# Moving GpSimd's share of the expert loop's weight subtracts to VectorE

## The chip, the cores and the metric

The kernel runs on one core of a Trainium2 chip. The metric is the device time of one execution in microseconds; the runs shown are three, with their median.

## The reference, cut to what matters

One layer of a streaming encoder over 2048 tokens of width 1024, in float32:

```
h = x + W_out [ Retention(n) ; RWKV7(n) ],   n = rms_norm(x) @ W_in
xn = rms_norm(h)
per token: one of 4 groups (argmax), then the 2 best of its 8 experts, weights = softmax(top 2) * group probability
y[token] += weight * ( silu(xb @ w_gate[e]) * (xb @ w_up[e]) ) @ w_down[e]      # 32 experts, 1024 -> 512 -> 1024
out = rms_norm_final(h + y)
```

The change lies in the part with the 32 experts, all of whose weights (6 MB each) are read once.

## The kernel before, in words

The kernel has three parts one after another: the mixers (to about 1500 us of the span), the tables of the routing, and the expert loop with the final norm behind it. Products are made of float32r parts: an operand is split into a high part, its cast to float32r, and a low part, the operand minus the high part, and three matmuls (high x high, low x high, high x low) are accumulated.

**Tiling of the expert loop** (lines 917 to 1223). Experts come in an order by size. Each has up to 128 tokens in a first block, and every second expert, by `more(e)`, a second block of 64 tokens. An expert is three stages: 0 the gate, 1 the up and 2 the down product; the list `stages` runs gate e, up e, down e-1, gate e+1 and so on. Each stage needs four weight chunks of 128 x 1024 float32 (512 KB).

**A chunk** is loaded by SP's queue into one of 8 buffers `raw` (line 903), cast on ScalarE (line 913) into the high half of one of 12 buffers `hl`, and the low half is written by a subtract `raw - hl` (line 914). Which engine casts and which subtracts is read from `SPLITS`, one string per kind of stage and one word per chunk: `a` or `v` (ScalarE or VectorE) for the cast, `p` or `v` (GpSimd or VectorE) for the subtract. The first six chunks are made ahead of the loop and don't use the table. Inside a stage four chunks are made, the last two of the next stage and the first two of the one behind it.

```
917: SPL = [[(V if a == "v" else SC, GP if b == "p" else V) for a, b in p.split()] for p in SPLITS]
913: (SC.copy if hi is SC else hi.tensor_copy)(hl[:, 0], raw)
914: lo.tensor_tensor(hl[:, 1], raw, hl[:, 0].bitcast(F32), op=ALU.subtract)
936: CH[si].append(chunk(*((SC, V) if first else SPL[stages[si][1]][c])))
```

**A stage**, in the order of the code: the first block's results of the stage before are taken from PSUM (`evict`); one chunk is made; the second block's matmuls of the stage before and its results (`rest`, where there is one); three chunks are made; additions that are due; then the stage's own matmuls in two halves. After each half of an up stage stand the transposes of half of the next expert's rows (`turn`, L1025), after those of a gate stage the transposes of the hidden rows (`hidden_turn`, L1125 for the first block, L1033 for the second). A transpose goes to one of two PSUM banks `tp`, which alternate; ScalarE casts it (L172) and VectorE subtracts (L173), and then the bank is free for the next transpose.

**GpSimd** has in the loop its share of the subtracts, the gathers of each expert's rows (`gather`, L1014, an indirect DMA into the one buffer `xb` of each block) and the additions of each expert's results to `h_d` (`add_rows`, L1147, an indirect DMA that adds). An addition waits for the one before it.

**Order.** In the loop the orders of TensorE, ScalarE, VectorE and GpSimd are those of the code (`manual_schedule`); SP's queue is ordered by a planner with priorities. A raw load is issued when the chunk eight places ahead of it has been made, and waits until that chunk's subtract has read the buffer.

Of the kernel before, what the change touches and what calls it, by code (L numbers as in the profile page):

```python
# [34 lines left out]
NFS = 6  # L35
FB = (2, 2, 2, 2, 2, 2, 2, 1, 1)
NRAW, NSP = 8, ((4, 0, 0), (4, 0, 0), (4, 0, 0))
SPLITS = ("av ap av vp", "av ap av av", "av ap av av")

N2 = 16  # L40

# [91 lines left out]
def build(tc, A, out, dbg=None, phases=3):  # L133
# [562 lines left out]
    if True:  # L696
# [219 lines left out]

        SPL = [[(V if a == "v" else SC, GP if b == "p" else V) for a, b in p.split()] for p in SPLITS]
        stages = [(0, 0), (0, 1)]
# [422 lines left out]
```

## Time and profile before

| | |
|---|---|
| three runs | 2427.48 us median (2424.75 to 2428.06) |
| profiled execution | 2430.18 us, of which the span 2428.4 |
| busy share of the span | TensorE 91%, VectorE 70%, GpSimd 48%, ScalarE 47% |
| weight subtracts (L914) | 259 on VectorE, 444.1 us; 125 on GpSimd, 332.6 us |
| weight casts (L913) | 353 on ScalarE, 352.0 us; 31 on VectorE |
| mean transfer rate | 187 GB/s over the span, 282 to 304 in most slices of the loop |
| granted TensorE clock | 0.951 mean |

Busy time counts an engine's instruction from its start to its end, and so also the time in which it stands still inside. A busy share of TensorE is not its peak. The three other engines take part in every stage of the expert loop, which runs from about 1567 to 2372 us of the span.

### The profile page before, as it was taken

The numbers are of one execution on the slowest core, as the hardware profiler recorded it, in microseconds if no ns is written. First come the engines' busy times: TensorE is split into PE (matmuls) and PEld (weight loads), VectorE is DVE, ScalarE is ACT, GpSimd is POOL, SyncE is SP. The second block draws the span as 40 slices with busy tenths as digits, with TensorE's granted clock in tenths as the row PEclk, the third lists the DMA queues.
The fourth block names the chain that finished last, engine by engine and source line by source line (L and its number), as shares of the span: only waits on it lengthen the run. The fifth ranks groups of instructions, "written<-read, shape, count | busy, mean of one in ns | idle before, by whom it ended". The sixth has DMA issues, their size and how long they took to land.

```text
span 2428.4 us, 36379 instructions
## 1 busy us (share of the span) xinstructions
PE 2207.2 (91%) x11816; PEld 1810.3 (75%) x11817; DVE 1710.4 (70%) x3500; ACT 1129.7 (47%) x1932; POOL 1161.3 (48%) x1530
## 2 busy tenths in 40 slices
PE   5999889998898989999879999699999999999990
PEld 4887778887787867877768888577777777777770
DVE  4477766878666877567775766768777787777875
ACT  4343433534434345333322222366666666666663
POOL 2036444354441575136542333466666666666650
PEclk9998999989999999999969999799999999999995
DMA  6643254432544335433234454488989999889978
GB/s 207 210 150 94 81 175 143 137 89 84 173 138 130 90 92 174 123 93 104 76 106 123 129 202 146 138 296 287 304 293 290 302 290 301 295 282 299 292 255 297
DMA packets 291298, 454.78 MB, mean 187 GB/s; under 512 B 93392, under 2 KB 164496, under 8 KB 291088
## 3 DMA queue, kind: packets, MB, share of 16 engines
q1 hardware_dynamic: 277136, 414.10, 51.6%
q0 software_dynamic: 13824, 37.80, 7.3%
q8 instruction: 94, 1.54, 0.3%
q14 instruction: 100, 0.82, 0.1%
q10 hardware_dynamic: 144, 0.52, 0.1%
HBM read 375.18 MB, written 81.85 MB: 188 GB/s over the span
## 4 chain that ended last, share of the span: by engine, by line
PE 47%; POOL 11%; DMA 7%; DVE 6%; issue 5%; ACT 3%; SPq 2%; POOLq 0%; DVEq 0%; ACTq 0%
PE acc L152 32%; PE pj L152 6%; POOL xl L488 5%; POOL tm L486 4%; PE pb L152 2%; PE tp L152 2%; ACT hl L913 1%; PE tp L1025 1%; DMA ln<-nl_d 1%; DVE hl L914 1%; PE psz L152 1%; DMA h_d<-yo,ti 1%; DMA xl_d<-xl 1%; PE psi L152 1%; SPq L490 1%
## 5 line engine op out<-in xcount | busy, mean ns | idle before, releaser
L152 PE MATMUL pj<-nT,whl 128*128 128x512 f32 x2496 | 626.4, 403 | 9.6 <-DVE nT L319 5.3
L914 DVE TENSOR_TENSOR hl<-raw,hl 128x1024 fp32r<-128x1024 f32 x259 | 444.1, 1745 | 142.6 <-ACT hl L913 142.6
L152 PEld LDWEIGHTS pj<-nT,whl 128*128 128x128 f32 x2496 | 464.9, 192 | 106.7 <-DVE nT L319 5.8
L152 PE MATMUL acc<-hl,xT 128*128 128x512 f32 (+1 forms) x2048 | 511.3, 402 | 0.0
L152 PEld LDWEIGHTS acc<-hl,xT 128*128 128x128 f32 (+1 forms) x2048 | 367.2, 183 | 100.8 <-ACT xT L172 0.2
L914 POOL TENSOR_TENSOR hl<-raw,hl 128x1024 fp32r<-128x1024 f32 x125 | 332.6, 2672 | 219.2 <-ACT hl L913 163.2
L913 ACT CAST hl<-raw 128x1024 fp32r<-128x1024 f32 x353 | 352.0, 1049 | 32.7 <-DMA raw<-in_wu_dram 26.9
L249 ACT CAST whl<-wraw 128x512 fp32r<-128x512 f32 x248 | 152.3, 618 | 304.8 <-PE pj L152 240.0
L250 DVE TENSOR_TENSOR whl<-wraw,whl 128x512 fp32r<-128x512 f32 x248 | 187.8, 760 | 146.1 <-ACT whl L249 141.7
L152 PE MATMUL acc<-hl,hT 128*128 128x512 f32 (+1 forms) x1024 | 249.6, 398 | 0.0
L486 POOL TENSOR_TENSOR tm<-xl,ln 128x60 f32<-128x60 f32 (+24 forms) x496 | 179.1, 361 | 105.6 <-DMA ln<-nl_d 69.0
L152 PEld LDWEIGHTS acc<-hl,hT 128*128 128x128 f32 (+1 forms) x1024 | 183.1, 181 | 51.7
L488 POOL TENSOR_TENSOR xl<-xl,tm 128x60 f32<-128x60 f32 (+24 forms) x496 | 187.5, 378 | 36.6
L152 PE MATMUL acc<-wo,mT 128*128 128x512 f32 x768 | 191.9, 401 | 0.0
L152 PEld LDWEIGHTS acc<-wo,mT 128*128 128x128 f32 x768 | 142.2, 191 | 28.5
L1147 POOL DMA_INDIRECT h_d<-yo,ti x48 | 107.5, 2239 | 53.8 <-DMA h_d<-yo,ti 40.5
L499 POOL COPY mbd<-pt 32x128 f32<-32x128 f32 x64 | 20.6, 321 | 226.5 <-DVE pt L464 199.4
L152 PE MATMUL pj<-whl,nT 128*128 128x256 f32 x768 | 118.6, 305 | 0.2 <-DVE gs L600 0.2
L152 PEld LDWEIGHTS pj<-whl,nT 128*128 128x128 f32 x768 | 105.9, 207 | 2.7 <-DVE gs L600 0.4
L464 DVE TENSOR_TENSOR pt<-pb,cst 64x512 f32<-64x512 f32 x128 | 88.0, 687 | 24.9 <-PE pb L152 23.1
L1014 POOL DMA_INDIRECT xb<-xt_d,ti x48 | 75.1, 1564 | 33.4 <-PE tp L1025 22.8
L172 ACT CAST xT<-tp 128x512 fp32r<-128x512 f32 x80 | 46.0, 589 | 80.7 <-PE tp L1025 65.7
(447 smaller groups left out, 3283.7 us busy)
## 6 DMA issues: line engine op xcount, KB each, us to landing
raw<-in_wg_dram SPq DMA_DIRECT2D x128, 512.0 KB, 4.7
raw<-in_wu_dram SPq DMA_DIRECT2D x128, 512.0 KB, 6.6
raw<-in_wd_dram SPq DMA_DIRECT2D x128, 512.0 KB, 6.7
wraw<-in_win_dram SPq DMA_DIRECT2D x208, 256.0 KB, 3.1
tr<-pf_d SPq DMA_DIRECT2D x80, 256.0 KB, 3.1
pf_d<-ev SPq DMA_DIRECT2D x52, 256.0 KB, 2.9
x<-in_xt_dram SPq DMA_DIRECT2D x32, 256.0 KB, 5.2
pf_d<-x SPq DMA_DIRECT2D x32, 256.0 KB, 4.2
```

The lines of the kernel that those rows point to most:

```text
L152: PE.matmul(o, l, r, start=start, stop=stop)
L172: SC.copy(dst_h, ps)
L249: SC.copy(hl[:, 0], raw)
L250: V.tensor_tensor(hl[:, 1], raw, hl[:, 0].bitcast(F32), op=ALU.subtract)
L464: V.tensor_tensor(pt[zs, i:i + 2, :, z ^ h], psp[h][zs].rearrange("p (f c) x -> p f c x", f=2), maskp[zs, None, None, :].to_broadcast([64, ...
L486: GP.tensor_tensor(tv, xl[:, 0:r, t:t + 1].to_broadcast([128, r, n]), ln[:, t:t + 1, t + 1:32].to_broadcast([128, r, n]), op=ALU.mult)
L488: GP.tensor_tensor(xl[:, 0:r, t + 1:32], xl[:, 0:r, t + 1:32], tv, op=ALU.add)
L490: SY.dma_start(xl_d[u].rearrange("l (r q) t -> q l r t", q=4)[q], xl[q * 32:(q + 1) * 32])
L913: (SC.copy if hi is SC else hi.tensor_copy)(hl[:, 0], raw)
L914: lo.tensor_tensor(hl[:, 1], raw, hl[:, 0].bitcast(F32), op=ALU.subtract)
L1014: return GP.indirect_dma_start(out=xbs[b], out_offset=None, in_=xt_d, in_offset=bass.IndirectOffsetOnAxis(ap=ti[b][:, e:e + 1], axis=0), b ...
L1147: GP.indirect_dma_start(out=h_d, out_offset=bass.IndirectOffsetOnAxis(ap=idx, axis=0), in_=y, in_offset=None, bounds_check=S + 127, comput ...
```

## The change

```
-SPLITS = ("av ap av vp", "av ap av av", "av ap av av")
+SPLITS = ("av av av av", "av av av av", "av av av av")
```

In all three kinds of stages the second chunk's subtract goes from GpSimd to VectorE. In a gate stage the fourth chunk's subtract does too, and its cast goes from VectorE to ScalarE. GpSimd keeps the gathers and the additions. Nothing else is edited.

## Rows read from the trace of the kernel before

**Rows 1.** Busy time in one stretch, 14 pairs of experts together; first line names the columns.
```profile
core 0: us, PE busy (x) PEld busy (x) DVE busy (x) ACT busy (x) POOL busy (x), PEclk, DMA share, GB/s
1596.79:2305.24 708.45, 691.29 (x3193) 532.71 (x3193) 531.75 (x462) 465.44 (x604) 461.82 (x196) 0.99 0.90 294
```
**Rows 2.** The same view, single pairs of experts.
```profile
1596.79:1645.64 48.85, 48.85 (x229) 37.86 (x229) 32.42 (x33) 33.03 (x44) 32.96 (x14) 1.00 0.87 280
1645.64:1695.75 50.11, 49.09 (x229) 37.80 (x229) 38.70 (x34) 34.19 (x45) 33.20 (x15) 1.00 0.90 296
1747.52:1798.92 51.40, 50.63 (x229) 38.87 (x229) 37.16 (x34) 33.09 (x43) 31.94 (x14) 0.97 0.90 298
1848.76:1900.52 51.76, 49.08 (x230) 37.79 (x229) 40.41 (x34) 33.42 (x44) 34.45 (x15) 1.00 0.92 285
2305.24:2355.00 49.76, 49.76 (x231) 38.54 (x231) 38.43 (x35) 33.06 (x44) 29.88 (x12) 1.00 0.93 305
```
**Rows 3.** Waits of TensorE in these 14 pairs: us in total, times, longest.
```profile
PE tp L1025 <- DVE hT L173: 17.2, 12, 2.7
```
**Rows 4.** Timeline of one gate and up stage: start, us, instruction, idle before it.
```profile
1837.14 4.76 POOL L914 TENSOR_TENSOR hl<-raw,hl 128x1024 fp32r<-128x1024 f32 x2
1838.54 3.89 ACT L913 CAST hl<-raw 128x1024 fp32r<-128x1024 f32 x4
1839.62 7.83 DVE L914 TENSOR_TENSOR hl<-raw,hl 128x1024 fp32r<-128x1024 f32 x3 [3.47 <-ACT hl L913]
1842.51 2.72 POOL L914 TENSOR_TENSOR hl<-raw,hl 128x1024 fp32r<-128x1024 f32 x1 [0.61 <-ACT hl L913]
1847.38 1.01 DVE L173 TENSOR_TENSOR hT<-tp,hT 128x512 fp32r<-128x512 f32 x2
1848.11 0.66 PE L1025 MATMUL tp<-ct,xb 128*128 128x128 f32 x4 [0.77 <-DVE hT L173]
```
**Rows 5.** The instructions of line 914: duration in ns, minimum/median/maximum.
```profile
L914 DVE TENSOR_TENSOR hl<-raw,hl x259: 1202/1220/7474, 1544.9 to 2360.9; 128x1024 fp32r<-128x1024 f32 x130
L914 POOL TENSOR_TENSOR hl<-raw,hl x125: 2347/2669/3427, 1570.4 to 2355.4; 128x1024 fp32r<-128x1024 f32 x125
```
**Rows 6.** Groups of VectorE in the 14 pairs: busy us, mean ns, idle before.
```profile
L914 DVE TENSOR_TENSOR hl<-raw,hl 128x1024 fp32r<-128x1024 f32 x224 | 390.9, 1774 | 126.3 <-ACT hl L913 126.2
L913 DVE CAST hl<-raw 128x1024 fp32r<-128x1024 f32 x28 | 19.2, 686 | 0.0
```
**Rows 7.** Timeline of the up and down stages before that.
```profile
1827.03 2.36 DVE L914 TENSOR_TENSOR hl<-raw,hl 128x1024 fp32r<-128x1024 f32 x2 [1.64 <-ACT hl L913]
1827.97 0.60 PE L1025 MATMUL tp<-ct,xb 128*128 128x128 f32 x4
1828.98 2.68 POOL L914 TENSOR_TENSOR hl<-raw,hl 128x1024 fp32r<-128x1024 f32 x1 [2.71 <-ACT hl L913]
1829.53 1.29 DVE L173 TENSOR_TENSOR xT<-tp,xT 128x512 fp32r<-128x512 f32 x2
1837.76 2.96 PE L152 MATMUL acc<-hl,xT 128*128 128x512 f32 x12
```
**Rows 8.** Timeline of ScalarE in the two down stages of a pair.
```profile
1806.61 2.13 ACT L913 CAST hl<-raw 128x1024 fp32r<-128x1024 f32 x2 [2.89 <-DMA raw<-in_wu_dram]
1837.26 1.39 ACT L1139 ACTIVATE yo<-acc,ws 128x512 f32<-128x512 f32 x2 [2.37 <-PE acc L152]
```
**Rows 9.** GpSimd's indirect DMAs: durations, two in the timeline, median us to landing.
```profile
L1147 POOL DMA_INDIRECT h_d<-yo,ti x48: 1432/2384/3606, 1619.7 to 2376.6; - x48
2371.20 1.43 POOL L1147 DMA_INDIRECT h_d<-yo,ti  x1 [5.25 <-DMA h_d<-yo,ti]
1835.43 1.67 POOL L1014 DMA_INDIRECT xb<-xt_d,ti  x1 [0.30 <-PE acc L152]
xb<-xt_d,ti POOLq DMA_INDIRECT x42, 7.4
```
**Rows 10.** Waits of SP's queue in the loop: us in total, times, longest.
```profile
SPq L903 <- POOL hl L914: 153.2, 91, 4.0
```

## The prediction

> **What bounds the kernel now.** I read the page first: TensorE is busy 91% of the span, and nine tenths or more of every slice of the expert loop but its ends. So I cut the loop into pairs of experts (the gates, ups and downs of one expert with the 64-row part and one without) and read busy time and clock in each. Over 14 whole pairs TensorE works 691.3 of 708.45 us [rows 1], which leaves at most a few per cent to win. The pairs are not alike [rows 2]: one runs without any idle TensorE, in 48.85 us at clock 1.00; six take 49.84 to 50.11 and four 51.1 to 51.8 us with TensorE idle for 0.8 to 2.7; three take 51.0 to 51.4 because their clock is 0.97. Each of those three follows one of the long idles (three of the four 51 us pairs have such a pair behind them). I take that as the price of the idle time, part of which comes back one pair later as clock. Waits of TensorE come next: one line holds all idle time inside the stretch, 17.2 us in 12 waits, the transposes of the next expert's rows (L1025) waiting for VectorE's low part of the transposed hidden rows (hT, L173), which frees their PSUM bank [rows 3].
>
> Why VectorE is late is seen in the timeline of one such place [rows 4]. ScalarE makes four casts in 3.89 us. VectorE then has three subtracts, and takes 7.83 us for them, because GpSimd is subtracting at the same time: 1837.14 to 1841.90, and again 1842.51 to 1845.23. VectorE's first hT subtract begins only at 1847.38, and the transposes, due at 1848.11 - 0.77 = 1847.34, wait. The durations say the same: a VectorE subtract has minimum 1.202 and median 1.220 us, but its longest record is 7.474 and its mean 1.774 [rows 5, 6]. It is short when GpSimd doesn't subtract, and waits out GpSimd's instruction when it does. So VectorE is late there through the other engine's 2.67 us instructions, not through its own amount of work.
>
> **The change part by part.**
> GpSimd loses 125 subtracts, 112 of them in the 14 pairs: 8 for each pair at 2.669 us median, 21.4 us of GpSimd per pair.
>
> VectorE gains those 8 and loses the two casts per pair (28 of 0.686 us [rows 6]). A subtract without GpSimd's beside it costs between 1.202 (minimum) and, if the long ones had another cause, 1.774 us. I take the median, 1.22, because more than half of the records lie there while GpSimd's gathers and additions go on as they will afterwards. Per pair before: busy 531.75/14 = 38.0, of which subtracts 390.9/14 = 27.9, casts 19.2/14 = 1.4, the rest 8.7 [rows 1, 6]. After: 24 x 1.22 + 8.7 = 38.0 us of a 48.85 us pair, 78%. Eight more instructions cost VectorE nothing in total.
>
> ScalarE gains the two casts per pair, about 1 us each (four in 3.89 [rows 4]): 2 us per pair on an engine busy 465.4/14 = 33.2 us. Both land ahead of a wait: in one half of the pair ScalarE stands 2.89 us for the raw load of the next up chunk, in the other 2.37 us for the down accumulation [rows 8]. Hidden there; if that cover were gone, the casts behind would come 1 us later, for chunks that are multiplied a whole stage (some 8 us) later. The subtract of that chunk, which followed VectorE's own cast, now waits for ScalarE's; behind it on VectorE stand the subtracts of the next two chunks, which wait for later casts anyway.
>
> What stands behind the added subtracts on VectorE's queue. At the place that stalls [rows 4], the four subtracts follow the casts: the first cast ends near 1839.59, so 1839.62 + 4 x 1.22 = 1844.50, and the hT subtract ends at 1845.2 where it is due at 1847.34: 2.1 us to spare instead of 0.8 late. The other side of it: the subtract that GpSimd does at 1828.98 [rows 7] comes to stand in front of VectorE's two xT subtracts, which start at 1829.53 now. Three subtracts from 1827.03 end at 1830.7, so xT is 1.2 us later and done by 1832.0. Its reader is the next gate, at 1837.76: 5.8 us are left. Elsewhere a subtract comes earlier by what it waited for GpSimd.
>
> The loads are released earlier as well. A raw buffer is free when its subtract has read it, and 91 waits of SP's queue, 153.2 us, end with a GpSimd subtract [rows 10]. After the change these end with a 1.22 us instruction instead of a 2.67 us one that stands behind an addition. SP's order of loads doesn't change.
>
> GpSimd's gathers and additions keep their order and lose the subtracts in between, so they start no later. I cost this at nothing: TensorE doesn't wait for them now. An addition takes 1.43 us with VectorE idle and 2.384 at the median in the loop [rows 9]; even six indirect DMAs per pair at the longest, 3.606, are 21.6 of 48.85 us.
>
> Outside the loop: the first six chunks are subtracted on VectorE already, and the last additions start behind the last down results, so nothing moves there but with the loop.
>
> **Sum.** 14 pairs at 48.85 are 683.9 instead of 708.45: -24.55 us, of which 17.2 is idle time that TensorE shows and some 7 is the lower clock and the refilling after each idle. Other pairs: the one before the stretch has no idle that this line causes, in the last one I count 0. The profiled execution took 2430.18 us (span 2428.4 and 1.8 around it); with 24.5 less, 2405.7. The runs shown have the median 2427.48, 2.7 lower, so the same difference gives 2403.0.
>
> **Rivals.**
> A. Only part of the idle time goes. With all chunks in VectorE's order, a subtract that waits for a late cast holds everything behind it; a third of these waits stood on GpSimd before, and VectorE already waits 126.2 us for casts [rows 6]. For: VectorE will be 78% busy with some 9 us of such waits per pair. Against: the replay above leaves 2 us at the place that counts. If half of the saving is lost, -12: 2415.
>
> B. The loads become the bound. The pairs move 294 x 708.45 = 208 MB, 14.9 MB each, at 294 GB/s and 0.90 of the DMA engines' time [rows 1]. At 48.85 us that is 304 GB/s and about 0.93. For: that is close to full. Against: a late pair held 305 GB/s at 0.93 while TensorE was busy all the time [rows 2]. If 300 GB/s were the most that lasts, a pair takes 49.5 us: 1.07 less than the mean 50.60, times 15.5 pairs = -16: 2411.
>
> C. The other side, VectorE's price: the long subtracts are long for another reason. If all 24 took 1.774, VectorE would need 24 x 1.774 + 8.7 = 51.3 us per pair, more than the 50.60 of now, and become the bound: 15.5 x 0.7 = +11 at the least, 2438, and more with its waits for casts on top. It decides from a mean of (50.60 - 8.7)/24 = 1.75 us. Against it stands the median, 1.220, and that in rows 4 the long ones end a subtract's length behind GpSimd's.
>
> D. The other side, the gathers: VectorE's subtracts hold up the descriptors that GpSimd writes. Row: 1.43 us for an addition with VectorE idle, 2.384 typically. If an indirect DMA had to wait for a whole run of four subtracts, 4.9 us, an addition and the gather behind it would take 2 x (4.9 + 1.43) = 12.7 us from the end of the transposes that free the buffer (1827.97 + 0.60 [rows 7]); landing 7.4 later [rows 9] is 1848.7 against 1847.34: 1.4 us for each of 31 experts, +43 on the floor of 2403: 2446. It decides when a gather comes more than 4.5 us later than today (1835.43 + 7.4 = 1842.8). Against: GpSimd's records show no wait of four subtracts, 3.606 being the longest.
> The Trainium skill (SBUF — State Buffer, "Who interferes with whom") says that a copy or cast can take the whole port pair from GpSimd, while it only infers that a two-input tensor_tensor leaves descriptor writing alone. By that rule D does not happen and the sum stays 2403; the trace agrees only in part, since 2.384 is not 1.43.
>
> E. The change does nothing that counts. The edit moves work between engines whose order is written by hand, but SP's order is the planner's; if its loads came later by what the subtracts come earlier, ScalarE's casts would wait instead and the idles stay: 2427.
>
> **How the numbers follow.** The forecast 0.62 (its own range 2398 to 2409); A 0.13; B 0.10; E 0.06; C 0.04; D 0.05. Faster by over 0.2% (4.9 us, about what a measurement tells from no change): forecast, A and B, 0.85. Same 0.06. Slower 0.09. The range from 2397 to 2420 takes in A and B with the forecast's own spread and leaves out C, D, E. Predicted: 2403.
>
> **What would show it.** Right: VectorE's subtracts have a mean below 1.3 us and no record above 2.5; the wait of L1025's transposes for hT is gone or below 3 us; nearly all pairs take 48.8 to 49.0 us at clock 1.00; GpSimd is busy less than half as long in the loop. A shows as transposes still waiting for hT or xT with short subtracts; B as casts waiting for raw loads in every pair with the DMA share above 0.93; C as a mean near 1.7; D as transposes waiting for gathers. The forecast is wrong if TensorE stays idle for more than 8 us in the same 14 pairs, or if the clock stays below 1.00 without idles.

## The result, and the profile after

| | before | after |
|---|---|---|
| median of the runs | 2427.77 us (2424.75 to 2434.31, 4 runs) | 2399.49 us (2395.73 to 2404.15, 4 runs) |
| ratio | | 0.9881, 95% interval 0.9851 to 0.991 |
| profiled execution, span | 2430.18, 2428.4 us | 2402.56, 2400.8 us |
| 14 pairs of experts | 708.45 us | 683.95 us |

The kernel is 28 us faster; forecast was 2403 us, 24.5 us less than before. The interval of the ratio stands for 22 to 36 us and holds both. The 14 pairs of [rows 1] lie between the same two matmuls of the program as before, which now stand at 1594.00 and 2277.95. Busy time of each engine in that stretch, in its first pair and in the pair behind it (the first line names the columns):

```profile
core 0: us, PE busy (x) PEld busy (x) DVE busy (x) ACT busy (x) POOL busy (x), PEclk, DMA share, GB/s
1594.00:2277.95 683.95, 683.95 (x3196) 530.15 (x3194) 518.78 (x547) 489.02 (x631) 113.75 (x84) 1.00 0.92 306
1594.00:1642.86 48.86, 48.86 (x232) 37.87 (x230) 37.06 (x40) 34.94 (x46) 7.66 (x6) 1.00 0.91 293
2277.95:2326.80 48.85, 48.85 (x229) 37.86 (x228) 37.06 (x40) 34.92 (x46) 6.34 (x4) 1.00 0.87 285
```

TensorE has no idle time at all here (17.2 us in [rows 3]), its clock is 1.00 throughout, and every pair takes what the one undisturbed pair of [rows 2] took. VectorE does 85 instructions more (547, not 462) in 13 us less [rows 1]. The instructions of line 914 (count, then minimum/median/maximum in ns), and their group in the stretch (busy us, mean ns, idle before it), show why:

```profile
L914 DVE TENSOR_TENSOR hl<-raw,hl x384: 1206/1219/1227, 1540.0 to 2331.8; 128x1024 fp32r<-128x1024 f32 x192
```
```profile
L914 DVE TENSOR_TENSOR hl<-raw,hl 128x1024 fp32r<-128x1024 f32 x337 | 393.5, 1219 | 106.0 <-ACT hl L913 106.0
```

The median is that of [rows 5], but the longest is now 1.227 us, not 7.474, and the mean has come down to the median from 1.774 [rows 6]. The place of [rows 4], in the pair of about the same time of the loop (timeline: start, us, instruction, idle before it):

```profile
1829.29 3.88 ACT L913 CAST hl<-raw 128x1024 fp32r<-128x1024 f32 x4
...
1830.35 4.63 DVE L914 TENSOR_TENSOR hl<-raw,hl 128x1024 fp32r<-128x1024 f32 x4 [1.78 <-ACT hl L913]
...
1834.90 1.05 DVE L173 TENSOR_TENSOR hT<-tp,hT 128x512 fp32r<-128x512 f32 x2
...
1837.69 0.59 PEld L1025 LDWEIGHTS tp<-ct,xb 128*128 128x128 f32 x4
```

Four subtracts in 4.63 us where three took 7.83. The first hT subtract (0.68 us) ends at 1835.58 and the transposes' first weight load comes at 1837.69: 2.11 us of room, where TensorE waited.

Of the 27.6 us between the two spans, 24.5 are these pairs, 2.5 lie ahead of them (the matmul that now begins at 1594.00 began at 1596.54) and 0.6 behind. The orders of TensorE's and SP's instructions are the same in both kernels, and so are the other engines' up to the loop. In the profiles of the runs below the same matmul begins between 1586.55 (e9) and 1596.52 us (e7), and not by the edit, so I take the 2.5 as spread between executions.

### The profile page after: what moved, and what is told of

Read it like the earlier page. It is cut to its first block, busy times and chain, and to the rows that moved or that the text cites. A ratio compares the mean times of both kernels' runs of the same rounds, so it can differ in the third digit from the quotient of the medians.

```text
span 2400.8 us, 36373 instructions
## 1 busy us (share of the span) xinstructions
PE 2196.5 (91%) x11816; PEld 1803.3 (75%) x11817; DVE 1698.5 (71%) x3594; ACT 1157.2 (48%) x1963; POOL 779.1 (32%) x1405
## 5 line engine op out<-in xcount | busy, mean ns | idle before, releaser
L913 ACT CAST hl<-raw 128x1024 fp32r<-128x1024 f32 x384 | 378.4, 1048 | 6.7 <-PE tp L152 3.0
L486 POOL TENSOR_TENSOR tm<-xl,ln 128x60 f32<-128x60 f32 (+24 forms) x496 | 173.8, 350 | 105.2 <-DMA ln<-nl_d 60.4
L488 POOL TENSOR_TENSOR xl<-xl,tm 128x60 f32<-128x60 f32 (+24 forms) x496 | 195.3, 394 | 36.6
L1147 POOL DMA_INDIRECT h_d<-yo,ti x48 | 80.1, 1670 | 299.3 <-ACT yo L1139 180.1
L1014 POOL DMA_INDIRECT xb<-xt_d,ti x48 | 49.5, 1031 | 369.6 <-PE tp L1025 288.0
L152 PE MATMUL pb<-ar,bk 64*128 64x128 f32 x512 | 76.3, 295 | 5.2 <-DVE pt L464 3.7
```

The costliest lines, as they stand in the source:

```text
L152: PE.matmul(o, l, r, start=start, stop=stop)
L486: GP.tensor_tensor(tv, xl[:, 0:r, t:t + 1].to_broadcast([128, r, n]), ln[:, t:t + 1, t + 1:32].to_broadcast([128, r, n]), op=ALU.mult)
L488: GP.tensor_tensor(xl[:, 0:r, t + 1:32], xl[:, 0:r, t + 1:32], tv, op=ALU.add)
L1014: return GP.indirect_dma_start(out=xbs[b], out_offset=None, in_=xt_d, in_offset=bass.IndirectOffsetOnAxis(ap=ti[b][:, e:e + 1], axis=0), b ...
L1147: GP.indirect_dma_start(out=h_d, out_offset=bass.IndirectOffsetOnAxis(ap=idx, axis=0), in_=y, in_offset=None, bounds_check=S + 127, comput ...
```

## The experiments

**One half of the change each.** The edit moves two things: the second chunk of every stage, and the gate's fourth chunk with its cast. e1 moves only the fourth chunk, e2 only the second ones.

```
e1  SPLITS = ("av ap av av", "av ap av av", "av ap av av")
e2  SPLITS = ("av av av vp", "av av av av", "av av av av")
```

> Only the gate's fourth chunk is changed (cast on ScalarE, subtract on VectorE); the second chunk of every stage stays on GpSimd, so GpSimd keeps 94 of 125 subtracts. Theory T (two or three GpSimd subtracts in a row hold VectorE's subtracts past the time at which hT's bank is due): at the place that stalls only one GpSimd subtract is left in front of VectorE's, so TensorE's 17.2 us of waits for hT fall below 4 us although many VectorE subtracts stay long; time 2402 to 2409. Rival S (each GpSimd subtract costs its share, 24.5 us / 8 per pair): 2 of 8 gone, 6 us gained, 2421.

> The other part alone: the second chunk of every stage goes to VectorE, the gate's fourth chunk keeps its VectorE cast and GpSimd subtract (31 left). Theory T: one GpSimd subtract per expert is left and never two in a row, so the waits for hT go below 2 us; time 2398 to 2405. Rival S: 6 of 8 gone, 18 us gained, 2409. Rival K (VectorE's cast, not the subtract, is what delays): the waits for hT stay at half or more, 2415.

Measured: e1 2399.91 us, ratio 0.9886 (0.9868 to 0.9904); e2 2403.27, 0.9893 (0.9874 to 0.9911). TensorE has no wait for hT in either, and the 14 pairs take 683.95 us in both. Line 914 in e1, VectorE and GpSimd:

```profile
L914 DVE TENSOR_TENSOR hl<-raw,hl x290: 1206/1218/2284, 1534.4 to 2325.9; 128x1024 fp32r<-128x1024 f32 x145
...
L914 POOL TENSOR_TENSOR hl<-raw,hl x94: 2393/2853/3090, 1560.7 to 2322.0; 128x1024 fp32r<-128x1024 f32 x94
```

Either half is worth the whole, within the intervals; e1 even lies 2 us below what was expected. A price for each GpSimd subtract (rival S) would have given 2421 for e1 and 2409 for e2. Rival K falls for e2, where the cast stays on VectorE. With 94 GpSimd subtracts left in e1, VectorE's longest is 2.284 us.

**Shut-out or data flow.** Did VectorE's subtracts get long because GpSimd's ran beside them, or was the kernel late because GpSimd delivered its low parts late? In both runs all the subtracts that count are on VectorE, and GpSimd works beside them on a scratch tile: in e3 it does a subtract at each of its old 125 places, in e4 three memsets. The edit, cut to what differs:

```
 lo.tensor_tensor(hl[:, 1], raw, hl[:, 0].bitcast(F32), op=ALU.subtract)
+if extra:                       # the chunks that GpSimd had before
+    hh = hl[:, 0].bitcast(F32)
+    GP.tensor_tensor(DUM, hh, hh, op=ALU.subtract)             # e3
+    for _ in range(3): GP.memset(DUM, 0.0)                     # e4, in its place
```

> All subtracts on VectorE as after the change, and GpSimd repeats its old 125 subtracts into a scratch tile that nobody reads (its inputs are the chunk's high part). Theory T (the two engines' subtracts shut each other out): VectorE's subtracts get long again, with 24 instead of 16 per pair exposed: VectorE's mean above 1.6 us, its need per pair near 51 us, waits for hT back; time 2430 to 2480, not below before. Rival L (the gain came from low parts being ready earlier, GpSimd's 2.67 us latency in the flow of data): nobody waits for the scratch, so 2398 to 2406.

> As the run with the scratch subtracts, but GpSimd does three memsets of 128x1024 in place of each (it writes SBUF and reads nothing; about 0.95 us each by the trace, 2.85 us together). Theory T with the shut-out on reading: VectorE's subtracts stay near 1.22 us and the time at 2398 to 2406. Rival Q (any busy GpSimd delays, by its queue or by writing): subtracts long or gathers late, 2420 or more.

Measured: e3 2482.88 us, 1.0216 (1.0197 to 1.0235), a little above what was expected; e4 2406.54, 0.9909 (0.9894 to 0.9924), 0.5 us above its range. TensorE's longest waits in e3's loop (us, times, longest) and VectorE's largest group there (busy, mean ns, idle before it); lines stand a few numbers lower down in these kernels:

```profile
PE tp L1031 <- DVE hT L173: 37.3, 14, 2.8
```
```profile
L916 DVE TENSOR_TENSOR hl<-raw,hl 128x1024 fp32r<-128x1024 f32 x358 | 577.5, 1664 | 50.5 <-ACT hl L915 50.5
```

Nobody reads the scratch tile, and only one cast waits for GpSimd to have read a chunk (0.2 us), yet the subtracts are long again (mean 1.664) and the kernel is slower than before: it is not GpSimd's latency in the flow of data (rival L) but the two engines' instructions shutting each other out. With memsets in the same places they don't. The instructions of both in e4:

```profile
L916 DVE TENSOR_TENSOR hl<-raw,hl x384: 1206/1218/1226, 1537.5 to 2331.1; 128x1024 fp32r<-128x1024 f32 x192
...
L919 POOL MEMSET dum<- x375: 952/956/1553, 1527.6 to 2321.1; 128x1024 f32 x188
```

So a busy GpSimd alone costs VectorE nothing here; one that subtracts, and so reads its operands from SBUF (in e3 one tile as both of them), does. The Trainium skill (SBUF — State Buffer, "Who interferes with whom") has this as a rule: a VectorE instruction with two SBUF inputs contends with a GpSimd instruction that reads SBUF, not with one that only writes it. These two runs agree with it: a mean of 1.664 us against at most 1.226. The intervals of e4 and of the change overlap, and e4's 14 pairs take 683.95 us too.

**The gate's fourth chunk taken apart.** From the kernel before, e5 moves only its subtract, e6 only its cast.

```
e5  SPLITS = ("av ap av vv", "av ap av av", "av ap av av")
e6  SPLITS = ("av ap av ap", "av ap av av", "av ap av av")
```

> As the kernel before, but the subtract of the gate's fourth chunk goes to VectorE, which keeps its cast too (GpSimd keeps the 94 second chunks). Theory T (two GpSimd subtracts in a row are what stalls): the waits for hT go below 3 us; time 2398 to 2406. Rival K (the cast on VectorE is what delays, and the earlier run gained by moving it to ScalarE): 2415 or more.

> As the kernel before, but the cast of the gate's fourth chunk goes to ScalarE; its subtract stays on GpSimd, which so keeps all 125. Theory T: two GpSimd subtracts still follow each other behind the gather at the place that stalls, so the waits for hT stay at 10 us or more; time 2415 to 2430. Rival K: waits gone, 2398 to 2406.

Measured: e5 2404.08 us, 0.9902 (0.9886 to 0.9918); e6 2404.05, 0.9898 (0.9884 to 0.9913). For e6 my theory was wrong. Its 125 GpSimd subtracts and VectorE's long ones are all there, and two still follow each other at the place that stalled; the wait is nearly gone anyway, as rival K had it. But K fails in e5, where VectorE keeps the cast and TensorE has no wait for hT. Neither theory fits both runs. Of e6: the wait for hT, line 914, and the timeline of such a place.

```profile
PE tp L1025 <- DVE hT L173: 1.7, 6, 0.8
```
```profile
L914 DVE TENSOR_TENSOR hl<-raw,hl x259: 1206/1221/6344, 1539.1 to 2334.4; 128x1024 fp32r<-128x1024 f32 x130
...
L914 POOL TENSOR_TENSOR hl<-raw,hl x125: 2368/2665/3419, 1564.4 to 2330.5; 128x1024 fp32r<-128x1024 f32 x125
```
```profile
1825.21 4.76 POOL L914 TENSOR_TENSOR hl<-raw,hl 128x1024 fp32r<-128x1024 f32 x2
...
1827.07 1.39 ACT L1139 ACTIVATE yo<-acc,ws 128x512 f32<-128x512 f32 x2 [1.43 <-PE acc L152]
...
1836.60 1.01 DVE L173 TENSOR_TENSOR hT<-tp,hT 128x512 fp32r<-128x512 f32 x2
1837.33 0.66 PE L1025 MATMUL tp<-ct,xb 128*128 128x128 f32 x4 [0.19 <-DVE hT L173]
```

The wait goes with the moment at which GpSimd's subtracts start. Time at this place is best counted from the moment at which ScalarE takes the down results from PSUM (L1139), because TensorE releases that. GpSimd's two subtracts start 1.86 us ahead of it here; in the place of [rows 4] they started 0.12 us ahead (1837.14 against 1837.26 in [rows 8]). With them hT's subtract comes earlier, and what is left late is 0.19 us.

The kernel before shows the same within itself. Its 14 places are of three kinds. In two of them GpSimd's subtracts start 2.1 us ahead, and TensorE doesn't wait; in eight they start 0.1 us ahead to 0.1 behind, and it waits 0.77 to 1.03 us; in four they start 1.6 us behind, three in a row, and it waits 2.7. One place of the first kind and one of the last:

```profile
1633.03 5.63 POOL L914 TENSOR_TENSOR hl<-raw,hl 128x1024 fp32r<-128x1024 f32 x2
...
1635.12 1.39 ACT L1139 ACTIVATE yo<-acc,ws 128x512 f32<-128x512 f32 x2 [2.37 <-PE acc L152]
...
1645.04 0.60 PE L1025 MATMUL tp<-ct,xb 128*128 128x128 f32 x4
```
```profile
1734.10 1.39 ACT L1139 ACTIVATE yo<-acc,ws 128x512 f32<-128x512 f32 x2 [2.38 <-PE acc L152]
...
1735.73 7.12 POOL L914 TENSOR_TENSOR hl<-raw,hl 128x1024 fp32r<-128x1024 f32 x3
1736.45 9.74 DVE L914 TENSOR_TENSOR hl<-raw,hl 128x1024 fp32r<-128x1024 f32 x3 [3.46 <-ACT hl L913]
...
1746.86 0.66 PE L1025 MATMUL tp<-ct,xb 128*128 128x128 f32 x4 [2.68 <-DVE hT L173]
```

The one place of e6 where the two start only 0.16 us ahead (near 2220 us) waits 0.77 us, as in the kernel before. The order is not strict: three places of e6 where they start 1.3 to 1.5 us ahead have no wait at all. GpSimd's subtracts are late by what stands ahead of them in its queue: in the four worst places of the kernel before, an addition of 3.4 to 3.6 us and a gather. Before the change GpSimd also stood 44.7 us in 14 waits of the loop for VectorE's cast of the fourth chunk; in e6 that cast is on ScalarE. That this handover alone made GpSimd late was not tried by itself.

**How much room there is.** The kernel after, with scratch subtracts on VectorE: e7 one in each stage (6 per pair of experts), e8 three and e9 two, only right ahead of hT's subtract (6 and 4 per pair). The edit, cut to what differs:

```
+hh = hl[:, 0].bitcast(F32)
+for _ in range(extra):     # e7: 1 at the second chunk of every stage; e8, e9: 3, 2 at the second down chunk
+    V.tensor_tensor(DUM, hh, hh, op=ALU.subtract)
```

> The kernel after, and VectorE subtracts each stage's second chunk once more into a scratch tile that nobody reads (6 more subtracts per pair of experts). It measures how much room VectorE has left. Theory T (only what stands in front of hT's subtract counts, with 2.1 us to spare): 38.0 + 6 x 1.22 = 45.3 us of 48.85 per pair, and one more subtract before hT leaves 0.9 us; time 2398 to 2408. Rival W (VectorE's waits for casts, some 8 us per pair, come on top: 53 us needed): VectorE is the bound, 15.5 x 4.3 more, about 2465.

> The kernel after, and VectorE makes three scratch subtracts in a row behind the second down chunk, that is right ahead of hT's subtract: 6 per pair of experts, as many as in the run that cost nothing, but all in this one place. Theory T (the one deadline of the bank of hT): room 2.10 us in every second gate stage, 3 x 1.135 used, so TensorE waits 1.3 us there 15 times, 20 us, with refilling and some slow-clock pairs 2420 to 2430. Rival N (VectorE's total work counts, not the place): the same 6 per pair, 2398 to 2408.

> The same with two scratch subtracts (4 per pair). Theory T: 2.10 - 2 x 1.135 leaves -0.17 us, so waits of about 0.2 us in 15 places, 3 us in all; time 2400 to 2410. Rival N: 2398 to 2406, without any waits for hT.

Measured: e7 2402.41 us, 0.9892 (0.9875 to 0.9909); e9 2406.34, 0.992 (0.9898 to 0.9942); e8 2426.61, 1.000 (0.9983 to 1.0017). Fourteen pairs in e7 and in e8, and e8's wait:

```profile
1596.50:2280.45 683.95, 683.95 (x3195) 529.99 (x3194) 606.40 (x631) 489.06 (x631) 165.41 (x84) 1.00 0.94 305
```
```profile
1592.71:2296.91 704.20, 687.16 (x3194) 529.14 (x3193) 610.96 (x631) 488.76 (x630) 133.67 (x84) 1.00 0.90 298
```
```profile
PE tp L1031 <- DVE hT L173: 17.0, 14, 1.2
```

VectorE works 606 and 611 us in the two, 84 scratch subtracts in each; e7 costs nothing, e8 gives the whole gain back. Only the place differs. In e7 VectorE is busy 89% and hT's subtract still has 0.96 us before the deadline: the first hT subtract starts at 1838.56, the weight load comes at 1840.20.

```profile
1838.56 1.02 DVE L173 TENSOR_TENSOR hT<-tp,hT 128x512 fp32r<-128x512 f32 x2
...
1840.20 0.59 PEld L1031 LDWEIGHTS tp<-ct,xb 128*128 128x128 f32 x4
```

Rival N (total work) and W (waits for casts on top) fall. e9 shows the 3 us that theory T expected: its 14 pairs take 686.48 us, 2.5 more than after the change. The waits of TensorE's matmuls don't show it, since it is the weight load ahead of the transposes that waits, in each of the 14 places:

```profile
1586.55:2273.03 686.48, 686.48 (x3196) 529.09 (x3193) 576.78 (x603) 487.44 (x631) 130.74 (x84) 1.00 0.92 304
```
```profile
PEld tp L1031 <- DVE hT L173: 5.5, 14, 0.4
```

e8 has the idle time of the kernel before (17.0 and 17.2 us) and is still 4.25 us shorter over the pairs; its waits in the pairs are at most 1.2 us and the clock is 1.00. Another 4.7 us of its time is one wait at the end of the loop, of the last expert's transposes for VectorE (e9 has 2.2 us there).

## Why the prediction was right

The direction, the place and the size held, step by step.

- *The floor.* 14 pairs at 48.85 us, 683.9, were forecast; 683.95 was measured.
- *VectorE.* 38.0 us per pair was forecast at 1.22 us a subtract; 518.78/14 = 37.06 was measured at 1.219. 337 subtracts of 1.219 us add up to 410.8, but neighbours overlap a little at their ends and 393.5 us are busy; that is the difference.
- *The deadline.* 2.1 us to spare was forecast, 2.11 measured; e7 to e9 spend it in known steps: one subtract leaves 0.96 us, two cost 0.18 us a pair, three 1.2 us of waiting.
- *ScalarE.* 35.2 us per pair forecast, 489.02/14 = 34.9 measured; the casts are hidden. Its waits for raw loads went down from 28.9 us to 3.6 us. The prediction expected the loads to be released earlier; that this is the cause is not shown, for e1, with 94 GpSimd subtracts left, has 3.9 us.
- *The clock.* 7 of the 24.55 us were put down to refilling and the lower clock behind long idles. e8 bears that out: the same idle time in short pieces costs 20.25 us, in the kernel before, with four waits of 2.7 us and three pairs at 0.97, 24.5. In the kernel before the granted clock fell to its lower level (0.50, that is 1.2 of 2.4 GHz) three times in these pairs, for 3.4 us each and each time at the end of a 2.7 us wait or within 1.4 us of it (the fourth such wait had no fall behind it). Pairs with a 0.77 us wait take 51.40 us with such a stretch and 49.85 without. Of the 7 us some 4.7 are thus the clock and the rest the refilling. One stretch:

```profile
1748.20:1751.60 3.40, 3.40 (x10) 2.57 (x9) 3.40 (x3) 0.00 (x0) 0.29 (x1) 0.50 0.97 247
```

- *Rivals.* A: no wait for hT or xT is left. B: the pairs move 306 GB/s at 0.92 of the DMA engines' time, and casts hardly wait. C: e3 made the long subtracts come back with GpSimd's instruction, so they need no other cause. E: SP's order did not change.
- *D* rested on a wrong reading. I took an addition's 2.384 us, against 1.43 with VectorE idle, as the delay by VectorE's subtracts. With 125 more of them the median addition takes 1.595 us and the gather 1.066 (1.651 before); what made the additions longer before stays open. The delay that D feared does exist, for gathers (see the last section), but after the change no gather of the loop from 1590 us on runs beside a weight subtract:

```profile
L1147 POOL DMA_INDIRECT h_d<-yo,ti x48: 1424/1595/2398, 1605.8 to 2348.6; - x48
...
L1014 POOL DMA_INDIRECT xb<-xt_d,ti x48: 937/1066/1079, 1554.4 to 2281.7; - x48
```

What was too simple is why VectorE was late. The prediction named the shut-out, which e3 shows, and read the place from one of its 14 instances, but did not ask how little was missing. e1, e2, e5 and e6 show a deadline: the bank of hT was missed by 0.8 to 1.0 us in eight pairs, by 2.7 in four and not at all in two, and each of four quite different edits to what stands ahead of it earned back all or nearly all. In e6 even the shut-out went on and only its start came earlier. The whole change was not needed for its gain.

None of these kernels is faster than the change beyond its interval: in e1, e2, e5 and the change the pairs are at TensorE's own 48.85 us, and moving subtracts can't shorten them further.

## What to carry to other kernels

An engine's long records beside a short median ask for the timeline of its neighbour: here one engine's instruction stood waiting for the other's, and the time counted as busy. Look for the deadline that is missed, by how much, and what stands in front of it; the gain is what the deadline costs, not the time of the work that is moved, and a small part of the change may earn all of it. Work added to an engine that is busy 76% of the time is free or dear by its place in the queue: the same 84 instructions cost nothing spread out and 20 us in front of the deadline.

## What was not expected of the hardware

A gather that runs beside VectorE's subtracts is slower. After the change all 43 gathers of the loop from 1590 us on run with no weight subtract beside them, 1.07 us at the median; in e7 a scratch subtract falls on each of them, and the median is 2.11. In the kernel before, the seven gathers without one took 1.08 us at most, the 33 beside at least 0.5 us of one 1.77 at the median. So the inference quoted under D in the prediction, that such subtracts leave the writing of descriptors alone, is not borne out by these gathers. It cost e7 nothing, because nothing waits for them.

The shut-out goes both ways, and can last for several instructions. In the kernel before, a VectorE subtract that had begun 0.7 us behind the first of three GpSimd subtracts took 7.47 us and ended behind all three. In e3 a GpSimd subtract, 2.424 us at the median, took up to 10.184: in each of the 14 places one began 0.4 us ahead of a row of seven VectorE subtracts and ended behind them all.
